# Second feed-forward half of a hybrid layer: direct products over all 512 tokens instead of the seven-product scheme

## Chip, cores and metric

The kernel runs on one core of one Trainium2 chip. The metric is the device time of one execution in microseconds; the kernel before takes 1804.71 us (median of three runs, 1804.62 to 1808.05).

## What is computed

One layer of a diffusion backbone on 512 latent tokens with 256 context tokens, 1,024 features, all in float32: a feed-forward half step, a token mixer (gated DeltaNet and pooling), a second feed-forward half step on the latents alone, and a last RMSNorm. The part that matters here is the second half step and the norm behind it:

```python
def swiglu(h, w_in, w_out):
    g, u = jnp.split(h @ w_in, 2, axis=-1)
    return (jax.nn.silu(g) * u) @ w_out

x = x + mx[5] * mix_x
x = x + 0.5 * mx[8] * swiglu(modulate(rmsnorm(x, norm3_w[i]), mx[6], mx[7]), ffn2_w_in[i], ffn2_w_out[i])
...
return rmsnorm(x, final_norm_w)
```

`w_in` is 1024 x 5632 (2,816 columns for g, 2,816 for u), `w_out` 2816 x 1024.

## The kernel before

Activations lie with the feature on the partition: a tile is 128 features by the tokens. A float32 product is made of three float32r products: each operand is split into a high part (a cast, on ScalarE) and a low part (operand less high part, a subtraction, on VectorE), and TensorE adds high x high, high x low and low x high in PSUM. `split_act` (lines 187 to 189) does this for activations, `halves` (lines 114 to 121) for up to four feature tiles of 128 weight columns (`whi`, `wlo`, four buffers each), `weights` (107 to 112) loads 128 columns of a matrix into a staging buffer `stg` (two of them) by one DMA from SyncE's queue and calls `halves` twice. `job` (123 to 134) is one tile of 128 output features over all tokens: for eight feature tiles, 24 matmuls with 512 columns in one PSUM bank. `next_bank` hands out the eight banks, tagged b, g and a, in turn.

The mixer's last step is eight such jobs with `w_mix_out` (lines 1108 to 1113); each result is added to the residual `xl` (line 1111) and its square to `acc2` (`norm_acc`, 191 to 197), from which `rstd_rows` (199 to 217) makes the norm's factors.

The second half step then goes by pairs of feature tiles. The first pair (lines 1114 to 1128) is made by plain products of 256 columns (`side_by_side`, `plain`), while `modulated` and `blocks_of` make the normalised input; `combine_pair` (on POOL) makes the extra right-hand operands, block differences. All other products go by `quad` (lines 337 to 371): two tiles of 128 output features and two halves of 256 tokens form a 2 x 2 block product, done with seven products instead of eight. The left operands are sums and differences of weight blocks, made on POOL in `quad_weights` (from 292: `qs`, and `qst` in place) and then split by `halves` like any weights; the seven results are added up from PSUM by VectorE (lines 354, 358, 360, 365, 370) and copied by ScalarE (352), into tiles `q`. `ffn` (from line 419) runs the quads in three groups of pairs, `G2 = ((0, 3), (3, 7), (7, 11))`: per pair a quad for g, Silu (line 462), a quad for u, four multiplications (474), and `combine` (252 to 266) with the splits that make seven right-hand operands `ahi`, `alo` for the output product; at the first pair of a group it does the output product of the group before it (`project7`, from 428), four quads, added to `xl` at line 437. Every instruction goes to its engine in an order that the framework's scheduler sets when the program is built; each engine works its own list in that order, and a buffer's next writer waits for its last reader.

After the last output quads `finish` (lines 1141 to 1149) adds the squares, scales by the norm's weight (`xw`, ScalarE), transposes four blocks on TensorE (1148) and copies them to `ot`; then come the row sums (1155), the factor, the scaling and four DMAs to the output.

## Time and profile before

| | |
|---|---|
| runs | 1804.62, 1804.71, 1808.05 us |
| span of the profiled execution | 1807.2 us |
| its own time | not printed apart; of the three runs only 1808.05 isn't shorter than the span, 0.85 us more |
| TensorE, VectorE, ScalarE, POOL busy | 91%, 76%, 52%, 35% of the span |
| chain that ended last | TensorE 55%, VectorE 25%, issue 6%, ScalarE 5%, DMA 5% |
| mean granted TensorE clock | 0.961 |
| DMA | 184 MB, mean 102 GB/s |

How to read it: the shares are means over the whole program, in which the first half step, the mixer and the second half step have different limits. The span is counted from the first to the last instruction. TensorE's matmuls overlap: the time of one in a row (0.28 us and more) is longer than the distance from its start to the next, so rates are read from starts. PEclk is the granted clock, 1.00 for 2.4 GHz and 0.50 for 1.2 GHz.

### The profile page before, as it was taken

What the parts mean: (1) busy time and instruction counts of PE and PEld (TensorE: products, weight loads), DVE (VectorE), ACT (ScalarE), POOL (GpSimd) and SP (SyncE); (2) the same over time, 40 slices, a digit from 0 to 9 for tenths busy, and PEclk for the clock granted to TensorE, in tenths of its full rate; (3) what the DMA queues carried; (4) which work ended last, traced back from release to release, by engine and by line L of the source; (5) the groups of instructions that cost most, each with busy time, mean ns of one, the idle gap of its engine ahead of it and who ended that gap; (6) DMA issues with size and microseconds to landing.
All of it is one profiled execution on the core that took longest, in us unless ns stands there. A gap on an engine that the chain in (4) does not pass through costs nothing.

```text
span 1807.2 us, 34927 instructions
## 1 busy us (share of the span) xinstructions
PE 1649.1 (91%) x13432; PEld 1486.5 (82%) x13432; DVE 1365.7 (76%) x2647; ACT 943.9 (52%) x2088; POOL 632.3 (35%) x669
## 2 busy tenths in 40 slices
PE   6899999999999999899999999999987888888886
PEld 4798998989999778777877888777877888888886
DVE  5778888897878874457776778645549899899886
ACT  5533343434344465757777776564426444444454
POOL 2244434444534020332233321100005556555642
PEclk9999999999999999999999999999998999899988
DMA  9455455351212353522221212247431222222221
GB/s 272 117 147 160 133 144 156 110 161 62 76 59 71 117 169 120 130 64 60 53 59 47 67 40 66 59 132 224 129 105 48 77 88 83 82 82 85 79 82 59
DMA packets 250971, 184.06 MB, mean 102 GB/s; under 512 B 7008, under 2 KB 238133, under 8 KB 250677
## 3 DMA queue, kind: packets, MB, share of 16 engines
q1 hardware_dynamic: 250368, 181.65, 34.4%
q8 instruction: 106, 1.74, 0.4%
q14 instruction: 60, 0.49, 0.1%
q10 hardware_dynamic: 437, 0.18, 0.0%
HBM read 170.22 MB, written 11.58 MB: 101 GB/s over the span
## 4 chain that ended last, share of the span: by engine, by line
PE 55%; DVE 25%; issue 6%; ACT 5%; DMA 5%; POOL 2%; SPq 0%; POOLq 0%; ACTq 0%; DVEq 0%
PE b L132 12%; PE b L345 11%; PE g L345 7%; PE a L345 6%; DVE wlo L120 4%; DVE cv L583 2%; DVE q L474 2%; DVE alo L189 2%; PE b L279 2%; DVE t L257 2%; DVE xT L437 1%; PE a L708 1%; PE a L132 1%; PE b L150 1%; PE g L132 1%
## 5 line engine op out<-in xcount | busy, mean ns | idle before, releaser
L119 ACT CAST whi<-qst 128x512 fp32r<-128x512 f32 (+2 forms) x288 | 159.1, 554 | 164.7 <-PE b L345 66.7
L120 DVE TENSOR_TENSOR wlo<-qst,whi 128x512 fp32r<-128x512 f32 (+2 forms) x288 | 215.5, 757 | 16.7 <-ACT whi L119 16.4
L119 ACT CAST whi<-qs 128x512 fp32r<-128x512 f32 (+2 forms) x216 | 117.7, 554 | 171.4 <-POOL qs L309 82.1
L132 PE MATMUL b<-hhi,whi 128*128 128x512 f32 (+1 forms) x528 | 188.4, 386 | 0.0
L132 PE MATMUL b<-hlo,whi 128*128 128x512 f32 (+1 forms) x528 | 188.3, 385 | 0.0
L132 PE MATMUL b<-hhi,wlo 128*128 128x512 f32 (+1 forms) x528 | 187.7, 386 | 0.0
L308 POOL TENSOR_TENSOR qs<-qst 128x512 f32<-128x512 f32 (+2 forms) x72 | 92.7, 1287 | 253.1 <-DMA qst<-in_ffn_w_in_dram 70.2
L313 POOL TENSOR_TENSOR qs<-qst,qs 128x512 f32<-128x512 f32 (+2 forms) x72 | 87.4, 1214 | 198.1 <-DVE wlo L120 181.1
L119 ACT CAST whi<-stg 128x512 fp32r<-128x512 f32 x154 | 94.3, 620 | 112.7 <-PE b L132 70.4
L120 DVE TENSOR_TENSOR wlo<-qs,whi 128x512 fp32r<-128x512 f32 (+2 forms) x144 | 104.9, 728 | 49.7 <-ACT whi L119 49.4
L345 PE MATMUL b<-ehi,wlo 128*128 128x384 f32 (+1 forms) x240 | 84.3, 351 | 45.7 <-DVE wlo L120 45.7
L179 POOL TENSOR_TENSOR rs<-rs,mhalf 128x4 f32<-128x4 f32 (+2 forms) x13 | 14.0, 1077 | 294.6 <-DVE rs L177 279.0
L188 ACT CAST ahi<-q 128x384 fp32r<-128x384 f32 (+1 forms) x118 | 55.3, 473 | 118.1 <-DVE q L474 60.8
L583 DVE SCALAR_TENSOR_TENSOR cv<-raw,vec,cv 128x772 f32<-128x772 f32 (+1 forms) x96 | 100.4, 1046 | 11.6 <-ACT cv L581 8.3
L345 PE MATMUL g<-hhi,whi 128*128 128x384 f32 (+1 forms) x320 | 105.5, 330 | 2.5 <-ACT whi L119 2.5
L345 PE MATMUL g<-hhi,wlo 128*128 128x384 f32 (+1 forms) x320 | 103.6, 324 | 3.6 <-DVE wlo L120 3.6
L132 PEld LDWEIGHTS b<-hlo,whi 128*128 128x128 f32 x528 | 94.6, 191 | 14.9
L132 PEld LDWEIGHTS b<-hhi,whi 128*128 128x128 f32 x528 | 94.5, 191 | 14.9
L132 PEld LDWEIGHTS b<-hhi,wlo 128*128 128x128 f32 x528 | 94.0, 191 | 15.0
L345 PE MATMUL g<-hlo,whi 128*128 128x384 f32 (+1 forms) x320 | 103.6, 324 | 0.0
L120 POOL TENSOR_TENSOR wlo<-stg,whi 128x512 fp32r<-128x512 f32 x46 | 65.4, 1429 | 90.6 <-ACT whi L119 70.5
L312 POOL TENSOR_TENSOR qst<-qst 128x512 f32<-128x512 f32 (+2 forms) x72 | 95.6, 1327 | 0.6
(480 smaller groups left out, 5459.6 us busy)
## 6 DMA issues: line engine op xcount, KB each, us to landing
qst<-in_ffn_w_in_dram SPq DMA_DIRECT2D x80, 512.0 KB, 3.5
stg<-in_w_ada_dram SPq DMA_DIRECT2D x56, 512.0 KB, 4.6
stg<-in_w_mix_in_dram SPq DMA_DIRECT2D x49, 512.0 KB, 3.9
qst<-in_ffn_w_out_dram SPq DMA_DIRECT2D x40, 256.0 KB, 2.7
adx<-in_w_ada_dram SPq DMA_DIRECT2D x16, 512.0 KB, 7.1
qst<-in_ffn_w_out_dram SPq DMA_DIRECT2D x16, 512.0 KB, 3.8
crow<-cumd SPq DMA_DIRECT2D x16, 384.0 KB, 8.8
stg<-in_ffn_w_in_dram SPq DMA_DIRECT2D x8, 512.0 KB
```

The lines of the kernel that those rows point to most:

```text
L119: (first.copy if first is act else first.tensor_copy)(out=hi[:, :n], in_=w)
L120: second.tensor_tensor(out=lo[:, :n], in0=w, in1=hi[:, :n], op=ALU.subtract)
L132: pe.matmul(res[p][:, :m], lhsT=ww(i), rhs=hh(k)[:, o:o + m], start=(i == 0 and j == 0), stop=(i == n - 1 and j == 2))
L188: act.copy(out=hi, in_=src)
L189: dve.tensor_tensor(out=lo, in0=src, in1=hi, op=ALU.subtract)
L257: eng.tensor_tensor(out=t, in0=x, in1=y, op=ALU.subtract)
L279: pe.matmul(x, lhsT=ww(k), rhs=rhs(j, part, k), start=n + e == 0, stop=n + e == len(ks) + 1)
L308: pool.tensor_tensor(out=s1, in0=a21, in1=a22, op=ALU.add)
L312: pool.tensor_tensor(out=a21, in0=a11, in1=a21, op=ALU.subtract)
L313: pool.tensor_tensor(out=s2, in0=a12, in1=s2, op=ALU.subtract)
L345: pe.matmul(o, lhsT=ww[:, k], rhs=rhs(j, part, k), start=first and k + i == 0, stop=k + i == nh + 1, skip_group_check=not first)
L583: dve.scalar_tensor_tensor(out=cv[:, :n], in0=raw[:, t:t + n], scalar=tap[t], in1=cv[:, :n], op0=ALU.mult, op1=ALU.add)
```

## The change

The second half step no longer uses the seven-product scheme. `tile_weights` loads 128 columns into one of three staging buffers `fst` and splits them into `fhi` and `flo`, five buffers of a whole tile each. The normalised input is written straight into `xhi` and `xlo` (512 tokens each), by one VectorE, one ScalarE and one VectorE step per feature tile. The first two feature tiles' g and u (four weight tiles) are produced while the input comes out, with one 512-column matmul where there were two of 256; every other tile is one `job`. Features go in three groups of tiles, 0 to 7, 8 to 15, 16 to 21; `project_out` adds a group's share to the residual after the first tile of the next group. The helpers `job`, `side_by_side`, `split_act`, `norm_acc`, `rstd_rows` and `finish`'s steps are as before. POOL has no weight sums or block differences left in this half. All other parts of the diff remove comments only.

```diff
-    e2 = ctx.enter_context(tc.tile_pool(name="e2", bufs=1, reuse_waits="tile"))
-    ehi = e2.tile([128, 4 * LAT], F32R, name="ehi2")
-    elo = e2.tile([128, 4 * LAT], F32R, name="elo2")
-    mn_cm = tc.tile_pool(name="mn", bufs=1, reuse_waits="tile")
-    mn = mn_cm.__enter__()
+    mn = ctx.enter_context(tc.tile_pool(name="mn", bufs=1, reuse_waits="tile"))
+    fw = ctx.enter_context(tc.tile_pool(name="fw", bufs=1, reuse_waits="tile"))
+    w_in, w_out = a["ffn2_w_in"], a["ffn2_w_out"]
+    def tile_weights(src, k0, nk, c0):
+        stg = fw.tile([128, KT, 128], F32, tag="fst", name="fst", bufs=3)
+        sp.dma_start(out=stg[:, :nk], in_=src[k0 * 128:(k0 + nk) * 128, c0:c0 + 128].rearrange("(k p) m -> p k m", p=128))
+        hi = fw.tile([128, KT, 128], F32R, tag="fhi", name="fhi", bufs=5)
+        lo = fw.tile([128, KT, 128], F32R, tag="flo", name="flo", bufs=5)
+        for i in range(0, nk, 4):
+            c = slice(i, min(i + 4, nk))
+            split_act(stg[:, c], hi[:, c], lo[:, c])
+        return [(lambda k, w=w: w[:, k]) for w in (hi, lo)]
     for m in range(0, KT, 2):
         for e in range(2):
             r = job(weights(a["w_mix_out"], 0, KT, 128 * (m + e)), lambda k: zhi[:, k], lambda k: zlo[:, k], range(KT), ONLY, next_bank)["lat"]
             dve.scalar_tensor_tensor(out=xl[:, m + e], in0=r, scalar=eff[:, 3, m + e, 0:1], in1=xl[:, m + e],
                                      op0=ALU.mult, op1=ALU.add)
             norm_acc(mn, acc2, xl[:, m + e], m + e, LAT)
-    ws = [weights(a["ffn2_w_in"], 0, KT, c) for c in (0, 128)]
+    hp_cm.__exit__(None, None, None)
+    GROUPS = ((0, 8), (8, 16), (16, 22))
+    hp2 = ctx.enter_context(tc.tile_pool(name="hp2", bufs=1, side="right", reuse_waits="tile"))
+    x2_cm = tc.tile_pool(name="x2", bufs=1, side="right", reuse_waits="tile")
+    x2 = x2_cm.__enter__()
+    xhi = x2.tile([128, KT, LAT], F32R, name="xhi")
+    xlo = x2.tile([128, KT, LAT], F32R, name="xlo")
+    f0 = [tile_weights(w_in, 0, KT, c) for c in (0, FF, 128, FF + 128)]
     for k in range(KT):
         mod_scale(2, k, 7, R_N3)
     mod_gate(1, 8, True)
-    rb = rstd_rows(mn, acc2, ONLY)
-    rhs2 = products(LAT // 2, (ehi, elo))
-    t = {}
-    first = [[[bank(tag)[:, :LAT // 2] for _ in range(2)] for tag in "bg"]]
-    steps = side_by_side(ws, first[0], blocks(rhs2), PAIRED)
-    for n, k in enumerate(PAIRED):
-        t[k] = modulated(mn, rb, xl[:, k], k, 2, 6, ONLY, bufs=8)
-        blocks_of(t[k], k, LAT // 2, rhs2)
+    rb = rstd_rows(mn, acc2, ONLY)["lat"]
+    banks = [bank(tag) for tag in "aagg"]
+    steps = side_by_side(f0, [[b] for b in banks], lambda _, part, k: (xhi, xlo)[part][:, k], range(KT))
+    for k in range(KT):
+        t = mn.tile([128, LAT], F32, tag="nt", name="nt", bufs=2)
+        shift = mods[:, 48 + k, 0:1]
+        dve.scalar_tensor_tensor(out=t, in0=xl[:, k], scalar=eff[:, 2, k, 0:1], in1=rb, op0=ALU.mult, op1=ALU.mult)
+        act.activation(out=xhi[:, k], in_=t, func=AF.Identity, bias=shift)
+        dve.scalar_tensor_tensor(out=xlo[:, k], in0=t, scalar=shift, in1=xhi[:, k], op0=ALU.add, op1=ALU.subtract)
         next(steps)
-    first.append(plain(a["ffn2_w_in"], FF, blocks(rhs2), LAT // 2, tags="ab"))
-    for kp in range(4):
-        combine_pair(mn, t, kp, LAT // 2, rhs2, pool)
-    mn_cm.__exit__(None, None, None)
-    # ---- second half-step and final norm ----
-    with tc.tile_pool(name="fp2", bufs=1, reuse_waits="tile") as fp:
-        late = []
-
-        def room():
-            hp_cm.__exit__(None, None, None)
-            p = ctx.enter_context(tc.tile_pool(name="op", bufs=1, side="right", reuse_waits="tile"))
-            late.append(p)
-            late.append(p.tile([128, 4, D], F32, name="ot"))
-
-        def finish(m):
...
-        ffn(fp, a["ffn2_w_in"], a["ffn2_w_out"], rhs2, ONLY, G2, lambda m: xl[:, m, :],
-            lambda m, s: eff[:, 1, m, s:s + 1], finish, lambda: None, first, 2, room)
+    fp = ctx.enter_context(tc.tile_pool(name="fp2", bufs=1, reuse_waits="tile"))
+    hh = {}
+    def activated(f, g, u):
+        t = fp.tile([128, LAT], F32, tag="ht", name="ht", bufs=2)
+        act.activation(out=t, in_=g, func=AF.Silu)
+        dve.tensor_tensor(out=t, in0=t, in1=u, op=ALU.mult)
+        hh[f] = [hp2.tile([128, LAT], F32R, tag=n, name=n, bufs=10) for n in ("fhhi", "fhlo")]
+        split_act(t, *hh[f])
+    def project_in(f):
+        g, u = (job(tile_weights(w_in, 0, KT, c + 128 * f), lambda k: xhi[:, k], lambda k: xlo[:, k], range(KT), ONLY,
+                    next_bank)["lat"] for c in (0, FF))
+        activated(f, g, u)
+    def project_out(f0, f1, done):
+        for m in range(KT):
+            r = job(tile_weights(w_out, f0, f1 - f0, 128 * m), lambda k: hh[k][0], lambda k: hh[k][1], range(f0, f1), ONLY,
+                    next_bank)["lat"]
+            dve.scalar_tensor_tensor(out=xl[:, m], in0=r, scalar=eff[:, 1, m, 0:1], in1=xl[:, m], op0=ALU.mult, op1=ALU.add)
+            done(m)
+    for f in range(2):
+        activated(f, banks[2 * f], banks[2 * f + 1])
+    for i, (g0, g1) in enumerate(GROUPS):
+        for f in range(max(g0, 2), g1):
+            project_in(f)
+            if f == g0:
+                project_out(*GROUPS[i - 1], lambda m: None)
+    x2_cm.__exit__(None, None, None)
+    op = ctx.enter_context(tc.tile_pool(name="op", bufs=1, side="right", reuse_waits="tile"))
+    ot = op.tile([128, 4, D], F32, name="ot")
...
+    project_out(*GROUPS[-1], finish)
...
```

(What is left out after `project_out(*GROUPS[-1], finish)` and inside `finish` is as in the kernel before, line for line, but for the indentation and the pool's name.)

The scheduler sets each engine's order. The first place is VectorE in the middle of the half. Before, one pair in the second group (`q` from lines 474 and 260, `t` from 257 and 265: products and block differences; `alo`: their low halves; `wlo`: low half of a weight block for the next quad):

```order
L474 TENSOR_TENSOR q<-q 128x256
L257 TENSOR_TENSOR t_19581<-q 128x256
L370 TENSOR_TENSOR q<-q,b 128x256
L260 TENSOR_TENSOR q<-q 128x256
L474 TENSOR_TENSOR q<-q 128x256
L257 TENSOR_TENSOR t_19584<-q,t_19581 128x256
L189 TENSOR_TENSOR alo<-t_19581,ahi 128x256
L189 TENSOR_TENSOR alo<-q,ahi 128x256 x2
L189 TENSOR_TENSOR alo<-t_19584,ahi 128x256
L120 TENSOR_TENSOR wlo<-qst,whi 128x512
```

The same engine in the change, feature tiles 2 to 4 (`ht`: Silu(g) times u; `flo`: low half of half a weight tile; `fhlo`: low half of the activation):

```order
L189 TENSOR_TENSOR fhlo<-ht,fhhi 128x512 x2
L189 TENSOR_TENSOR flo<-fst,fhi 128x512 x8
L1153 TENSOR_TENSOR ht<-ht,b 128x512
L189 TENSOR_TENSOR flo<-fst,fhi 128x512 x2
L189 TENSOR_TENSOR fhlo<-ht,fhhi 128x512
L189 TENSOR_TENSOR flo<-fst,fhi 128x512 x2
L1153 TENSOR_TENSOR ht<-ht,b 128x512
```

Before, nine instructions of the pair stand ahead of a weight block; now each feature tile has one product and one split between the splits of two weight tiles, and the splits of four more tiles stand ahead of the first product.

The second place is TensorE where the first two feature tiles end (line 279, operand `xhi`) and the first jobs begin (line 132), in the change:

```order
L279 MATMUL g<-xhi,fhi 128x512
L279 MATMUL g<-xlo,fhi 128x512
L279 MATMUL g<-xhi,flo 128x512
L132 MATMUL b<-xhi,fhi 128x512
L132 MATMUL b<-xlo,fhi 128x512
L132 MATMUL b<-xhi,flo 128x512
L132 MATMUL b<-xhi,fhi 128x512
L132 MATMUL g<-xhi,fhi 128x512
```

Four matmuls of the job in bank b come first, then all of the job in a bank g, which still holds a result of the first 96 matmuls until ScalarE or VectorE has read it.

The third place is the end of TensorE's list in the change (`xw`: the scaled output, transposed by line 1187):

```order
L132 MATMUL a<-fhhi,fhi 128x512
L132 MATMUL a<-fhlo,fhi 128x512
L132 MATMUL a<-fhhi,flo 128x512
L1187 MATMUL b<-ident,xw 128x128 x8
L132 MATMUL b<-fhhi,fhi 128x512
L132 MATMUL b<-fhlo,fhi 128x512
L132 MATMUL b<-fhhi,flo 128x512
```

The transposes of two output tiles stand between the last matmuls of one job and the first of the last one; before, transposes stood in fours between the products of a quad, and the last eight behind all of them.

## Rows read from the trace of the kernel before

**Rows 1.** The page, part 1: busy us, share of the span, instructions by engine.

```profile
PE 1649.1 (91%) x13432; PEld 1486.5 (82%) x13432; DVE 1365.7 (76%) x2647; ACT 943.9 (52%) x2088; POOL 632.3 (35%) x669
```

**Rows 2.** Busy time by stretch: us, PE, PEld, DVE, ACT, POOL, PEclk, DMA, GB/s.

```profile
1302.80:1347.40 44.60, 44.60 (x192) 35.84 (x191) 21.72 (x32) 14.88 (x24) 0.00 (x0) 1.00 0.33 94
...
1358.90:1363.60 4.70, 4.63 (x21) 4.63 (x22) 4.65 (x9) 4.70 (x12) 3.35 (x5) 0.50 0.02 5
...
1358.90:1792.40 433.50, 373.06 (x2820) 365.50 (x2820) 390.82 (x608) 212.63 (x439) 238.50 (x175) 0.91 0.24 75
...
1528.70:1535.10 6.40, 6.40 (x57) 6.40 (x56) 6.33 (x11) 2.88 (x6) 4.34 (x4) 1.00 0.26 82
...
1540.00:1544.00 4.00, 4.00 (x19) 4.00 (x20) 3.94 (x9) 1.96 (x4) 0.00 (x0) 0.50 0.45 131
...
1769.00:1773.00 4.00, 4.00 (x22) 4.00 (x23) 4.00 (x4) 3.04 (x6) 3.92 (x3) 0.61 0.00 0
```

**Rows 3.** Waits from 1347 to 1808: us in total, times, longest us.

```profile
PE b L345 <- DVE wlo L120: 40.8, 11, 4.8
```

**Rows 4.** Timeline of TensorE around a pause: start us, us, instruction, wait before it.

```profile
1528.73 0.28 PE L345 MATMUL a<-hhi,whi 128*128 128x256 f32 x1
...
1535.19 0.28 PE L345 MATMUL b<-elo,whi 128*128 128x256 f32 x1
...
1539.98 0.58 PE L345 MATMUL b<-ehi,wlo 128*128 128x256 f32 x1 [4.51 <-DVE wlo L120]
...
1540.36 0.41 PE L345 MATMUL b<-ehi,whi 128*128 128x256 f32 x1
...
1544.41 0.36 PE L345 MATMUL g<-hlo,whi 128*128 128x256 f32 x1
```

**Rows 5.** Chain of waits through that pause: start us, us, engine, tile, line.

```profile
1535.16 1.41 DVE q L474
...
1536.57 1.41 DVE t L257
...
1539.32 0.61 DVE wlo L120
```

**Rows 6.** Chain of waits, the mixer's output projection, first and last of eight jobs.

```profile
1302.83 5.62 PE g L132 x24
...
1342.18 5.63 PE b L132 x24
```

**Rows 7.** Timeline of TensorE, last part of the projection before it, first and last.

```profile
1284.76 0.39 PE L132 MATMUL g<-yghi,wlo 128*128 128x512 f32 x1
...
1302.44 0.39 PE L132 MATMUL b<-yghi,wlo 128*128 128x512 f32 x1
```

**Rows 8.** Chain of waits from 1300 to 1810: a table load, matmuls on `ahi`.

```profile
1382.12 1.28 ACT L462
...
1460.66 1.08 PE g L345 x9
```

**Rows 9.** Groups by line, 1302.5 to 1347.5: busy us, mean ns, idle before.

```profile
L120 DVE TENSOR_TENSOR wlo<-stg,whi 128x512 fp32r<-128x512 f32 x16 | 11.0, 687 | 8.5 <-ACT whi L119 8.5
...
L119 ACT CAST whi<-stg 128x512 fp32r<-128x512 f32 x16 | 9.9, 621 | 25.8 <-PE b L132 13.4 <-PE a L132 6.8 <-PE g L132 5.5
...
L1111 DVE SCALAR_TENSOR_TENSOR xl<-b,eff,xl 128x512 f32<-128x512 f32 x3 | 2.3, 751 | 5.0 <-PE b L132 5.0
```

**Rows 10.** Loads of line 110, 1230 to 1350, from issue to landing.

```profile
DMA to landing us min/median/max: 3.0/3.4/3.9
```

**Rows 11.** Chain of waits at the start of the half.

```profile
1357.11 1.52 ACT nt L225 x2
...
1358.63 0.30 ACT hhi L188
...
1358.97 0.58 PE b L279
```

**Rows 12.** Timeline of TensorE, the last matmul of the half.

```profile
1792.19 0.28 PE L345 MATMUL b<-ahi,wlo 128*128 128x256 f32 x1
```

More of the change, by code (lines that the diff above doesn't have):

```diff
@@ L1128, in layer_kernel @@
-    for kp in range(4):
-        combine_pair(mn, t, kp, LAT // 2, rhs2, pool)
-    mn_cm.__exit__(None, None, None)
-    with tc.tile_pool(name="fp2", bufs=1, reuse_waits="tile") as fp:
-        late = []
-        def room():
-            hp_cm.__exit__(None, None, None)
-            p = ctx.enter_context(tc.tile_pool(name="op", bufs=1, side="right", reuse_waits="tile"))
-            late.append(p)
-            late.append(p.tile([128, 4, D], F32, name="ot"))
-        def finish(m):
-            p, ot = late
-            norm_acc(p, acc2, xl[:, m], m, LAT)
-            y = p.tile([128, LAT], F32, tag="xw", name="xw", bufs=2)
-            act.activation(out=y, in_=xl[:, m], func=AF.Copy, scale=vec[:, 0, R_NF + m:R_NF + m + 1])
-            b = bank()
-            for c in range(4):
-                pe.transpose(b[:, c * 128:(c + 1) * 128], y[:, c * 128:(c + 1) * 128], ident)
-            act.copy(out=ot[:, :, m * 128:(m + 1) * 128], in_=b.rearrange("p (c x) -> p c x", c=4))
-        ffn(fp, a["ffn2_w_in"], a["ffn2_w_out"], rhs2, ONLY, G2, lambda m: xl[:, m, :],
-            lambda m, s: eff[:, 1, m, s:s + 1], finish, lambda: None, first, 2, room)
+    rb = rstd_rows(mn, acc2, ONLY)["lat"]
@@ L1153, in layer_kernel, with finish @@
+    x2_cm.__exit__(None, None, None)
+    op = ctx.enter_context(tc.tile_pool(name="op", bufs=1, side="right", reuse_waits="tile"))
+    ot = op.tile([128, 4, D], F32, name="ot")
+    def finish(m):
+        norm_acc(op, acc2, xl[:, m], m, LAT)
+        y = op.tile([128, LAT], F32, tag="xw", name="xw", bufs=2)
+        act.activation(out=y, in_=xl[:, m], func=AF.Copy, scale=vec[:, 0, R_NF + m:R_NF + m + 1])
         b = bank()
         for c in range(4):
-            pe.matmul(b[:, c:c + 1], lhsT=acc2[:, c * 128:(c + 1) * 128], rhs=ones[:, 0:1])
@@ L1156, in layer_kernel @@
-        r = rstd_of(b[:, :4], 4, D)
-        ot = late[1]
-        for c in range(4):
-            if c % 2:
-                act.activation(out=ot[:, c], in_=ot[:, c], func=AF.Copy, scale=r[:, c:c + 1])
-            else:
-                dve.tensor_scalar(out=ot[:, c], in0=ot[:, c], scalar1=r[:, c:c + 1], scalar2=None, op0=ALU.mult)
-            sp.dma_start(out=out[0, c * 128:(c + 1) * 128, :], in_=ot[:, c])
+            pe.transpose(b[:, c * 128:(c + 1) * 128], y[:, c * 128:(c + 1) * 128], ident)
@@ new lines, in finish @@
+        act.copy(out=ot[:, :, m * 128:(m + 1) * 128], in_=b.rearrange("p (c x) -> p c x", c=4))
+    project_out(*GROUPS[-1], finish)
+    b = bank()
+    for c in range(4):
+        pe.matmul(b[:, c:c + 1], lhsT=acc2[:, c * 128:(c + 1) * 128], rhs=ones[:, 0:1])
+    r = rstd_of(b[:, :4], 4, D)
+    for c in range(4):
+        if c % 2:
+            act.activation(out=ot[:, c], in_=ot[:, c], func=AF.Copy, scale=r[:, c:c + 1])
+        else:
+            dve.tensor_scalar(out=ot[:, c], in0=ot[:, c], scalar1=r[:, c:c + 1], scalar2=None, op0=ALU.mult)
+        sp.dma_start(out=out[0, c * 128:(c + 1) * 128, :], in_=ot[:, c])
```

## Prediction, made before the changed kernel was run

> **What bounds the kernel now.** I read the engine totals first: TensorE is busy for 91% of the span, VectorE for 76% [rows 1]. An average over stages doesn't say what the second half waits for, so the table of stretches comes next [rows 2]. From 1358.9 to 1792.4 us, the feed-forward half itself, TensorE is busy for 373.06 of 433.50 us at a mean granted clock of 0.91, VectorE for 390.82: there VectorE is the fuller engine. The table of waits of that stretch names the place: TensorE stood 40.8 us before matmuls of bank b, 11 times, each time for `wlo` of line 120, the low half of a weight tile that VectorE splits off [rows 3]. The timeline shows one such pause [rows 4]: matmuls follow one another until 1535.19, the next starts at 1539.98, after 4.51 us of waiting. The chain of waits says what VectorE did meanwhile [rows 5]: the pair's multiplications and block differences (`q`, `t`, 1.4 us each though only 256 wide), and only after them `wlo`. They stand ahead of it in VectorE's order.
>
> The pause costs twice. After it the matmuls start 0.213 us apart instead of 0.117 [rows 4], because the granted clock of 1540.0 to 1544.0 is 0.50, the 1.2 GHz level, where 1528.7 to 1535.1 shows 1.00, the 2.4 GHz level [rows 2]. From 1540.36 to 1544.41 lie 19 such steps, then the distance is short again; at half rate for some 4.6 us some 2.1 us are lost, so a pause of 4.5 us costs about 6.6.
>
> **How 433 us are made up.** The seven-product scheme issues 2,796 matmuls of 256 columns here: 192 for the first pair by plain products, 20 quads of 84 for `w_in` (1,680), 4 quads of 63 and 8 of 84 for `w_out` (924). 55 steps lead from 1528.73 to 1535.19 [rows 4], 0.1174 us each: 2,796 x 0.1174 = 328 us at the full clock. TensorE's idle time is 433.5 - 373.1 = 60 us. The rest, 433.5 - 328 - 60 = 45 us, is half clock and the 32 transposes of the end. So 105 us of the stage are not matmuls at full speed.
>
> **What the change does, part by part.**
>
> 1. Matmuls: 44 tiles of `w_in` x 8 feature tiles x 3 = 1,056 and 8 x 22 x 3 = 528 for `w_out`, 1,584 of 512 columns. The same shape, from the same kind of job (one 512 KB weight load, two casts, two subtractions, 24 matmuls), runs just ahead of the stage, in the output projection of the mixer: eight jobs in a row of 5.62 or 5.63 us without a gap [rows 6], 0.2344 each, clock 1.00 for 44.6 us [rows 2]. 1,584 x 0.2344 = 371.3 us, **43 us more** matmul time than before. The rows bound this price: 79 starts from 1284.76 to 1302.44 (the projection before, operand `yghi`) are 0.2267 apart [rows 7], so down to 359.1; nine 256-wide matmuls on `ahi` take 1.08 us [rows 8], 0.24 per 512, so up to 380. I take 0.2344, of the nearest stage; nothing in the rows says why they differ. The Trainium skill (TensorE: Matmul & The Clock Gate, section "Back-to-back issue gap") gives N/2.4 + 2.5 ns, 216 ns for 512 columns; by it the sum would be 30 us lower. The trace disagrees by 19 ns a matmul, and the measurement decides.
>
> 2. VectorE and POOL: gone are the block differences and the sums of weights. VectorE keeps 136 subtractions of 512-wide weights at 0.687, 22 products, 22 splits and 24 residual updates of about 0.7 to 0.75 [rows 9]: some 142 us in 371. ScalarE: 136 + 22 casts at 0.62 and 22 Silus of about that, some 112 us. Per tile of 5.62 us VectorE needs about 2.1, ScalarE 1.9. In the new VectorE order the splits of four tiles stand ahead of the first product, splits run about four tiles ahead of their use, and a product that waits for TensorE does not make TensorE wait. I cost these edits at nothing; the cover is those four tiles, 22 us. If it were gone, a tile's cast, subtraction and hand-overs (about 1.7 us) would be bare.
>
> 3. Weight loads: as many bytes, 512 KB per 5.62 us, 93 GB/s. The mixer's output projection moves the same at 94 GB/s [rows 2] in packets half as long as those of the old `qst` loads, each landing in 3.0 to 3.9 us [rows 10]. Nothing. Five of the loads and their ten splits now run inside that projection: 10 x 0.69 us more on VectorE, which is busy 21.72 of 44.60 us there [rows 2]. Hidden, unless a weight load of the projection falls behind them; then one pause, up to 6.6.
>
> 4. Start: from the last matmul of the projection (1347.81) to the first of the half it takes 11.2 us, through norm and row factors [rows 11]. The new code has one ScalarE step where there were two in a row (`nt` x2, `hhi`): first matmul at about 1358.0, 0.9 earlier. VectorE and ScalarE then feed a feature tile about every 1.7 us, TensorE needs 2.8 for its 12 matmuls. The clock starts at 0.50 as before [rows 2]: 4.7 us of it, 2.1 lost. When the first 96 matmuls end, the banks g are free only after a table load (1.28 [rows 8]) and two Silus: 0.7.
>
> 5. End: eight jobs of 18 matmuls, with 28 of the 32 transposes between them (0.5 for four, 3.5 in all). Each needs its residual update and a ScalarE copy, some 2.5 us after its job; the order puts 9 to 18 matmuls between, but the last two rounds stand bare: waits of about 3.5 in all, and 2 for the clock that falls (it read 0.61 from 1769 to 1773, between the same rounds of the old end [rows 2]). From the last matmul's start, 1792.19, the old tail takes 15.0 to the span's end [rows 12]; its steps are the same.
>
> **The sum**: 10.2 + 371.3 + 2.1 + 0.7 + 3.5 + 3.5 + 2.0 = 393.3 after 1347.8, so the last matmul is at 1741.1, the span's end at 1756.1, against 1807.2: 51.1 less. Put otherwise, of the 105 us of pauses, half clock and transposes some 12 stay, and 43 are paid back in columns. The span is 2.5 above the median of the runs, 1804.7; 1804.7 - 51.1 = **1753.6 us**.
>
> **Rivals.**
> - *The matmul rate of the projection before.* If the rows at 0.2267 hold for the new operands, which lie like `yghi` in rows of 512 tokens, it is 12.2 less: 1741. For it: they are the one other stretch of this shape; against it: all 192 matmuls nearest to the change ran at 0.2344.
> - *No overhead at all.* At half clock 256 columns take 0.2132 [rows 4], just 256 / 1.2 GHz; at twice the clock 512 would take the same, 33.6 us less: 1720. No stretch in the trace shows it. The page's rule above belongs here, with 1724.
> - *A few pauses remain* (at the hand-over from the first 96 matmuls, at the two group borders, in the projection ahead, at the end): two to five of 6.6 us, 1767 to 1787. Against it: the projection had none in eight jobs, with only two tiles of look-ahead.
> - *Slower: TensorE pauses at the borders of jobs and falls to 1.2 GHz.* The place is the VectorE order where `ht` waits for a finished bank and the next `flo` stands behind it. If look-ahead fails there once a feature tile, 20 pauses cost 132 us: 1886. It decides from eight pauses on (8 x 6.6 = 53). For it: it is just what bounds the stage now. Against it: the four tiles of cover, VectorE at 2.1 of 5.6 us, and 44.6 us without a gap across eight banks. The Trainium skill (the same page, section "A second HAM failure mode: psum-queue depth-cycling") tells of a kernel at N = 512 whose clock swung as it cycled through PSUM banks. That rule speaks against this change; the trace disagrees, with clock 1.00 over eight such jobs.
>
> **How the numbers follow.** My forecast, 1744 to 1765, has 0.60: the sum, with the tail's waits gone or doubled. The faster rate has 0.15, no overhead 0.03, remaining pauses 0.15, something between those and no change 0.03, slower 0.04. 1737 to 1776 holds the forecast, the faster rate and about half of the pauses; 0.17 stays out. About 0.2% (3.6 us) is what a measurement of this kernel can tell from no change. Faster 0.95, same 0.01, slower 0.04.
>
> **What would show it.** Right: in the changed kernel the jobs of the half take 5.6 us for 24 matmuls, TensorE's waits for `flo` are near nothing, the clock reads 1.00 from about 1363 until the last rounds, VectorE is busy under half of the stage. Wrong: 5.44 or 5.76 us a job (rate), pauses of several us before a tile's first matmul (splits or loads), or the stretch 1303 to 1348 getting longer (the early loads).

## The result, and the profile after

The changed kernel took 1753.05 us (median of 4 runs, 1749.31 to 1756.71), the kernel before beside it 1806.38 (4 runs): a ratio of 0.9697, 95% interval 0.9673 to 0.9721. The forecast was 1753.6, faster. The profiled execution took 1756.71 us, its span is 1755.0, the longest of the four (the others 1747.6 to 1751.7).

The engine totals of the changed kernel, from its page, answer to [rows 1]:

```profile
PE 1653.5 (94%) x12220; PEld 1423.9 (81%) x12220; DVE 1119.0 (64%) x2254; ACT 842.6 (48%) x1851; POOL 390.8 (22%) x493
```

VectorE lost 247 us of work, POOL 242; TensorE's busy time is nearly the same (4 us more). The table of stretches (columns as in [rows 2]):

```profile
1307.60:1352.50 44.90, 44.90 (x192) 35.80 (x191) 25.49 (x39) 18.18 (x31) 0.00 (x0) 1.00 0.56 152
...
1358.00:1363.00 5.00, 3.18 (x5) 1.41 (x6) 2.70 (x5) 1.38 (x2) 0.00 (x0) 0.50 0.00 0
1384.00:1700.00 316.00, 316.00 (x1350) 253.88 (x1349) 112.69 (x176) 89.49 (x162) 0.00 (x0) 1.00 0.33 95
1735.00:1742.00 7.00, 4.88 (x23) 3.70 (x22) 1.44 (x2) 1.84 (x4) 0.00 (x0) 1.00 0.00 0
...
1358.00:1742.00 384.00, 379.28 (x1614) 302.74 (x1614) 138.71 (x217) 111.75 (x200) 0.00 (x0) 0.99 0.27 80
```

Over the half TensorE is busy for 379.28 of 384.00 us at clock 0.99, and from 1384 to 1700 without a break at 1.00; before, it was busy for 373.06 of 433.50 at 0.91 [rows 2]. VectorE needs 138.71 us of the half (390.82 before), POOL none (238.50). The early loads fall into the mixer's output projection (first row: 152 GB/s where there were 94), and TensorE has no gap there.

What is left of the pauses stands in the table of waits from 1300 to 1756 (us in total, times, longest), all of TensorE's entries; [rows 3] is gone:

```profile
PE b L1187 <- ACT xw L1184: 4.3, 3, 2.2
PE b L215 <- DVE diag L209: 2.3, 1, 2.3
PE b L205 <- DVE acc L197: 2.3, 1, 2.3
PE a L279 <- ACT xhi L1143: 1.6, 1, 1.6
```

The chain of waits shows the half from its first to its last matmul (start us, us, engine, bank, line, count):

```profile
1361.90 1.22 PE a L279 x2
...
1386.87 0.93 PE b L132 x4
1387.80 5.72 PE g L132 x24
1393.52 4.69 PE b L132 x20
...
1696.21 5.62 PE b L132 x24
1701.84 4.22 PE g L132 x18
...
1736.31 0.66 PE b L1187 x4
1736.96 4.23 PE b L132 x18
1741.19 0.02 issue
```

A job is 5.62 us, and one follows the other without a gap until 1733.59. In the profiled pair the half takes 1755.0 - 1352.58 = 402.4 us from the end of the mixer's projection, where it took 1807.2 - 1347.81 = 459.4 [rows 6]: 57.0 less. That the projection ended 4.8 us later hides a part of it in the spans. In the profiled runs below the same job ended between 1344.7 and 1355.3, so a few us of a difference in whole time can lie ahead of the half.

### The profile page after: what moved, and what is told of

The parts are those of the page before. It is cut to its first block, busy times and chain, and to the rows that moved or that the text cites. A ratio compares the mean times of both kernels' runs of the same rounds, so it can differ in the third digit from the quotient of the medians.

```text
span 1755.0 us, 31315 instructions
## 1 busy us (share of the span) xinstructions
PE 1653.5 (94%) x12220; PEld 1423.9 (81%) x12220; DVE 1119.0 (64%) x2254; ACT 842.6 (48%) x1851; POOL 390.8 (22%) x493
## 4 chain that ended last, share of the span: by engine, by line
PE 71%; DVE 14%; ACT 5%; DMA 5%; POOL 2%; issue 2%; SPq 0%; ACTq 0%; POOLq 0%; DVEq 0%
PE b L132 22%; PE b L345 9%; PE a L132 6%; PE g L132 6%; PE a L345 5%; PE g L345 5%; DVE cv L583 2%; PE b L279 2%; PE a L279 1%; PE g L279 1%; PE a L708 1%; ACT din L848 1%; DVE wlo L120 1%; DMA bg_dram<-bgate 1%; PE b L150 1%
## 5 line engine op out<-in xcount | busy, mean ns | idle before, releaser
L188 ACT CAST fhi<-fst 128x512 fp32r<-128x512 f32 (+1 forms) x136 | 77.7, 605 | 249.6 <-PE b L132 85.6
L189 DVE TENSOR_TENSOR flo<-fst,fhi 128x512 fp32r<-128x512 f32 (+1 forms) x136 | 87.3, 671 | 92.6 <-ACT fhi L188 92.4
L119 ACT CAST whi<-qst 128x512 fp32r<-128x512 f32 (+1 forms) x160 | 81.6, 512 | 106.5 <-PE b L345 43.2
L119 ACT CAST whi<-qs 128x512 fp32r<-128x512 f32 (+1 forms) x120 | 59.5, 512 | 115.2 <-POOL qs L309 76.2
L120 DVE TENSOR_TENSOR wlo<-qst,whi 128x512 fp32r<-128x512 f32 (+1 forms) x160 | 100.7, 639 | 10.1 <-ACT whi L119 10.0
L120 DVE TENSOR_TENSOR wlo<-stg,whi 128x512 fp32r<-128x512 f32 x100 | 68.2, 686 | 22.1 <-ACT whi L119 20.2
L120 DVE TENSOR_TENSOR wlo<-qs,whi 128x512 fp32r<-128x512 f32 (+1 forms) x80 | 49.0, 613 | 32.6 <-ACT whi L119 32.6
L132 PE MATMUL b<-xlo,fhi 128*128 128x512 f32 x160 | 63.4, 396 | 0.0
L132 PE MATMUL b<-xhi,flo 128*128 128x512 f32 x160 | 63.4, 396 | 0.0
L132 PE MATMUL b<-xhi,fhi 128*128 128x512 f32 x160 | 63.4, 396 | 0.0
```

Source lines behind the costliest of these rows:

```text
L119: (first.copy if first is act else first.tensor_copy)(out=hi[:, :n], in_=w)
L120: second.tensor_tensor(out=lo[:, :n], in0=w, in1=hi[:, :n], op=ALU.subtract)
L132: pe.matmul(res[p][:, :m], lhsT=ww(i), rhs=hh(k)[:, o:o + m], start=(i == 0 and j == 0), stop=(i == n - 1 and j == 2))
L188: act.copy(out=hi, in_=src)
L189: dve.tensor_tensor(out=lo, in0=src, in1=hi, op=ALU.subtract)
```

## The experiments

Theory as predicted: VectorE's work per pair stands ahead of the next split, so TensorE pauses and restarts at half clock; the change ends that and pays 43 us of columns. Rivals: fewer matmuls are the gain; the number of weight buffers is; POOL is. Ratios are to the kernel before on the same chip in the same session; the changed kernel's own is 0.9697.

| kernel | median us | ratio (95%) |
|---|---|---|
| changed, jobs in two halves of 256 | 1755.55 | 0.9701 (0.9686 to 0.9715) |
| before, no block differences | 1768.27 | 0.9777 (0.9761 to 0.9793) |
| before, six weight buffers | 1788.91 | 0.9879 (0.9863 to 0.9895) |
| before, no sums on POOL | 1724.22 | 0.9538 (0.9511 to 0.9565) |
| before, POOL's sums unread | 1821.96 | 1.0066 (1.0040 to 1.0091) |
| changed, POOL kept busy | 1763.29 | 0.9750 (0.9719 to 0.9781) |
| changed, operands moved | 1742.62 | 0.9626 (0.9599 to 0.9653) |
| changed, weights moved | 1741.10 | 0.9627 (0.9599 to 0.9655) |
| changed, both moved | 1748.55 | single run, no interval |
| mixed, seven products for `w_in` | 1754.31 | 0.9692 (0.9678 to 0.9707) |
| mixed, for the gate half only | 1745.61 | 0.9651 (0.9624 to 0.9677) |
| mixed, gate half, moved operands | 1743.99 | 0.9636 (0.9618 to 0.9654) |

The three kernels without block differences, without POOL's sums and with the sums unread compute something else in the half, from as many matmuls; only their times are read.

### Is it the number of matmuls?

```diff
+        for s in range(2):
+            c = slice(256 * s, 256 * s + 256)
+            for i, k in enumerate(ks):
+                for j, (ww, hh) in enumerate(((w[0], act_hi), (w[0], act_lo), (w[1], act_hi))):
+                    pe.matmul(b[:, c], lhsT=ww(i), rhs=hh(k)[:, c], start=(i == 0 and j == 0), stop=(i == n - 1 and j == 2))
```

> The changed kernel with each job's 512 tokens again as two runs of 256-column matmuls, one token half after the other in the same bank (1,488 of the 1,584 matmuls; the first 96 stay). Same columns, same splits and buffers, but 3,072 matmuls in place of 1,584. Theory (the gain is pauses and half clock that went): two matmuls of 0.117 take the place of one of 0.234, 5.6 us a job, no pauses, the time of the changed kernel, 1745 to 1760. Rival (the gain comes from half as many matmuls and weight loads on TensorE): a good part of the 50 us comes back, 1780 or more.

Measured 0.9701, the same as the changed kernel. Twice the matmuls and weight loads in these jobs cost nothing that the intervals show; that rival is out.

### Less work for VectorE, or more look-ahead?

The products that read the differences read plain blocks instead (left out), and the differences aren't made:

```diff
-                    combine(fp, g[0][0], g[0][1], g[1][0], g[1][1], n2, put, deep - 1)
+                    if final:
+                        combine(fp, g[0][0], g[0][1], g[1][0], g[1][1], n2, put, deep - 1)
```

> The kernel before, second half only, without the block differences of the activations and their splits; the products that would read them read one of the blocks instead (so the second half computes something else, with the same 2,796 matmuls). VectorE loses eight operations a pair, nothing else changes. Theory (VectorE's chain of a pair stands ahead of the next split, TensorE pauses and then runs at half clock): the waits for the low half of a weight tile shrink from 41 us to under 10, the clock of the half rises from 0.91 to 0.97 or more, 1740 to 1765. Rival (fewer matmuls and weight loads are the gain): the matmuls are as many as before, so 1795 to 1806. Rival (the number of split-weight buffers): the buffers are as before, so 1790 to 1806.

The other one takes two more `whi` and `wlo` buffers from the half's own pool:

```diff
+        more[1] += 1
+        p, nb = (more[0], 2) if more[0] and more[1] % 6 >= WB else (wp, WB)
+        hi = p.tile([128, 4, 128], F32R, tag="whi", name="whi", bufs=nb)
+        lo = p.tile([128, 4, 128], F32R, tag="wlo", name="wlo", bufs=nb)
```

> The kernel before, with six instead of four buffers for the split weights in the second half, nothing else. Theory (VectorE's work per pair, 390 of 433 us, and its order): VectorE has little idle time to run ahead in, so the gain is small, 1785 to 1806. Rival (the look-ahead in buffers is what lacks): the pauses of 4.5 us go, since two more products of 1.4 us are split ahead, 1750 to 1770.

Without the block differences some 40 us went, with the buffers 21.5: the first lies 3 us above the theory's range, the second inside it. But not every sign came as expected. Without the differences TensorE still waited 18.7 us for `wlo`, where under 10 were expected. With six buffers the wait of [rows 3] did go, as the rival had it; others took its place, mainly for VectorE's sums of the seven products (waits from 1340 to 1790):

```profile
PE a L349 <- DVE q L362: 23.8, 25, 2.0
```

So both the order and the look-ahead mattered, and VectorE stayed behind in either. What it did is the interesting part. Stretches of the run without differences, and its split (groups by line, 1359 to 1760: busy us, mean ns, idle before):

```profile
1347.00:1765.00 418.00, 365.47 (x2863) 350.05 (x2861) 375.56 (x541) 201.55 (x407) 248.65 (x178) 0.97 0.28 86
```

```profile
L120 DVE TENSOR_TENSOR wlo<-qst,whi 128x512 fp32r<-128x512 f32 (+1 forms) x128 | 144.8, 1136 | 7.5 <-ACT whi L119 7.1
```

Eight operations a pair are gone, and VectorE is still busy for 375.56 of 418 us: its split takes 1136 ns here, in a group with a few of 384 columns (932 in the same view of the kernel before); those of 128x512 alone take 1166 (936 before), where [rows 9] has 687. So the number of VectorE's operations is not all that filled it. Something made them long.

### What makes VectorE's operations long

The timeline of the kernel before through the pause of [rows 5], VectorE and then POOL (start us, us, instruction):

```profile
1533.98 1.18 DVE L260 TENSOR_TENSOR q<-q 128x256 f32<-128x256 f32 x1
1535.09 1.49 DVE L474 TENSOR_TENSOR q<-q 128x256 f32<-128x256 f32 x1
1536.50 1.48 DVE L257 TENSOR_TENSOR t<-q,t 128x256 f32<-128x256 f32 x1
1537.90 0.41 DVE L189 TENSOR_TENSOR alo<-t,ahi 128x256 fp32r<-128x256 f32 x1
...
1533.52 1.36 POOL L308 TENSOR_TENSOR qs<-qst 128x512 f32<-128x512 f32 x1
1534.96 1.33 POOL L309 TENSOR_TENSOR qs<-qs,qst 128x512 f32<-128x512 f32 x1
1536.25 1.44 POOL L312 TENSOR_TENSOR qst<-qst 128x512 f32<-128x512 f32 x1
```

Each of the three long operations ends 0.28 to 0.29 us after a POOL instruction does (1534.88, 1536.29, 1537.69), one after the other; from 1537.90, with POOL at rest, the same width takes 0.41.

The trace shows the same all through the half of the kernel before. From 1358.9 to 1792.4, 137 of VectorE's operations on two tiles of the on-chip memory took over 0.1 us longer than alone. Every one of them ended a fixed time after the end of a POOL instruction that fell inside it: 0.28 or 0.29 us at 256 columns, 0.41 or 0.42 at 384, 0.55 or 0.56 at 512. Of the 177 with one input in PSUM none was longer, though 95 of them ran beside POOL. (22 more two-tile ones overlapped a POOL instruction and kept their time.) So an operation that is held up stands still until POOL's instruction is over. The next two runs separate that from POOL's place in the chain of data.

First POOL's four sums and differences a quad are left out (parts of the edit):

```diff
+        if plain:
+            s1, s2 = a22, a12
+        else:
+            pool.tensor_tensor(out=s1, in0=a21, in1=a22, op=ALU.add)
...
-        pool.tensor_tensor(out=s2, in0=a12, in1=s2, op=ALU.subtract)
```

> The kernel before, second half only, without POOL's four sums and differences of weight blocks per quad; the products that would read them read plain blocks of the weights (so the second half computes something else, with the same 2,796 matmuls and the same number of splits, casts and block differences of activations). VectorE's instructions are the same to the last one; only POOL's busy time in the half falls, from 238 us to about 50. Theory (VectorE's own number of operations fills it): its 390 us stay, and the time stays within 10 us of the kernel before, 1795 to 1812. Rival (VectorE is slow because POOL works beside it: 128x256 operations take 0.41 us where POOL rests and 1.0 to 1.5 where it doesn't): VectorE's operations fall to 0.69 and 0.41, some 290 us in all, the pauses shrink to a third, 1745 to 1770.

Then they are made again, into a tile that nothing reads (two of the four):

```diff
+            d = tmp.tile([128, 4, 128], F32, tag="pd", name="pd", bufs=1)[:, :nh]
+            pool.tensor_tensor(out=d, in0=a21, in1=a22, op=ALU.add)
+            pool.tensor_tensor(out=d, in0=a12, in1=a11, op=ALU.subtract)
...
```

> The kernel before, second half only, with the plain blocks of weights as in the run without POOL's sums, but with POOL doing its four additions and subtractions per quad again, from the same tiles into a tile that nothing reads (so the second half computes something else). No product waits for POOL's results any more; POOL's work beside VectorE is back. Theory after the run without POOL's sums, contention (VectorE is slow while POOL works): VectorE's 128x256 operations are back at 1.0 us and more, the pauses come back, 1785 to 1810. Rival, dependence (the way from load over POOL's sums to the split was too long, with two buffers for a sum): the pauses stay away, 1720 to 1740.

Without POOL's sums the seven-product kernel takes 1724 us, 84 less than before, below even the rival's range, and the changed kernel's direct products are 29 slower than that. So the theory that VectorE's own number of operations fills it is out. With the sums back, read by nobody, it takes 1822, more than the kernel before and 12 above the range expected. So the dependence on the sums is worth little, and that they run beside VectorE is most of the 84 us. Stretches and groups (1359 to 1792) without the sums:

```profile
1347.00:1717.00 370.00, 347.07 (x2847) 341.51 (x2846) 305.31 (x627) 220.56 (x450) 60.40 (x50) 0.97 0.31 96
```

```profile
L120 DVE TENSOR_TENSOR wlo<-qst,whi 128x512 fp32r<-128x512 f32 x168 | 113.5, 685 | 16.7 <-ACT whi L119 15.4
...
L480 DVE TENSOR_TENSOR q<-q 128x256 f32<-128x256 f32 x30 | 12.6, 421 | 0.7
```

And with the sums unread, the same two views and the wait that is back:

```profile
1347.00:1820.00 473.00, 379.06 (x2873) 366.40 (x2871) 416.47 (x631) 222.41 (x453) 243.51 (x178) 0.92 0.25 76
```

```profile
L120 DVE TENSOR_TENSOR wlo<-qst,whi 128x512 fp32r<-128x512 f32 x164 | 165.0, 1019 | 11.4 <-ACT whi L119 11.3
L486 DVE TENSOR_TENSOR q<-q 128x256 f32<-128x256 f32 x30 | 24.8, 826 | 0.7
```

```profile
PE b L357 <- DVE wlo L120: 40.5, 10, 5.1
```

The same instructions on VectorE (627 and 631 in the two stretches) take 305 us beside a POOL that works for 60, and 416 beside one that works for 244. The wait of [rows 3], 40.8 us in 11 pauses, is there again with 40.5 in 10. One thing differs from the kernel before: TensorE now also waits 12.7 us, in 11 pauses, for weight splits that POOL makes itself (`wlo` from POOL), where the kernel before has no long wait for POOL. That is not VectorE's slowness, and may be why this run is slower than the kernel before.

Then the other way round, POOL busy in the changed kernel:

```diff
+        d = fw.tile([128, 512], F32, tag="pd", name="pd", bufs=1)
+        for i in range(3):
+            pool.tensor_tensor(out=d, in0=stg[:, 0:4].rearrange("p k m -> p (k m)"), in1=stg[:, 1:5].rearrange("p k m -> p (k m)"), op=ALU.add)
```

> The changed kernel with three additions of 128x512 on POOL for every weight tile of the half, into a tile that nothing reads: POOL works for about 4.3 of each 5.6 us. Theory of the prediction (splits run four tiles ahead, VectorE needs 2.1 of 5.6 us): even if VectorE's splits take 1.0 to 1.1 instead of 0.69 us it keeps ahead, 1750 to 1760, no pauses. Rival (a POOL that rests is the whole gain): the pauses come back, 1780 or more. If POOL does not slow VectorE at all, its split stays at 0.69 us here, and the rival of the run without POOL's sums has lost its reason.

Groups of this run by line (1359 to 1792), and its stretch behind the start:

```profile
L189 DVE TENSOR_TENSOR flo<-fst,fhi 128x512 fp32r<-128x512 f32 x118 | 133.3, 1160 | 43.2 <-ACT fhi L188 43.1
L189 DVE TENSOR_TENSOR fhlo<-ht,fhhi 128x512 fp32r<-128x512 f32 x22 | 35.7, 1627 | 0.0
L1156 DVE TENSOR_TENSOR ht<-ht,b 128x512 f32<-128x512 f32 x20 | 13.8, 688 | 54.3 <-PE b L132 54.3
```

```profile
1365.00:1738.00 373.00, 371.20 (x1586) 297.42 (x1585) 214.93 (x211) 108.11 (x195) 265.03 (x180) 1.00 0.28 82
```

Splits take 1160 and 1627 ns instead of 686 and 684. The product `ht`, of the same shape, one of whose inputs is a PSUM bank (`b`), takes 688 as in a quiet kernel: what POOL holds up is the operation that reads two tiles of the on-chip memory. The Trainium skill has this as a rule (SBUF — State Buffer, section "Who interferes with whom"): a VectorE instruction with two inputs in SBUF contends with a GpSimd instruction that reads SBUF, and one with at most one such input, outside the 2-port perf modes, does not; the port pair that the two engines share is an exclusive lock. The traces agree: 1160 against 688 ns here, and the ends 0.28 us behind POOL's in the pause.

The time rose by some 10 us only, 3 above the range of the look-ahead theory and far below the rival's 1780, for VectorE at 214.93 of 373 us keeps ahead. TensorE stood for 1.8 us in that stretch; the rest is mostly two waits, 5.8 us together, in the projection ahead, where early splits, 1.7 us long, stood before the projection's own. So a busy POOL is dear where VectorE is nearly full, and cheap where it isn't.

### Where a job's 5.62 us come from

In the traces a job of 24 matmuls takes 5.44 us on `yghi` and 5.62 on `hhi`, `xhi` and the activations. The first lie in a pool taken from the low end of the on-chip memory, like all weights; the others in one taken from the high end.

The edit moves the operands' two pools to the low end (`side="right"` is the high one):

```diff
-    hp2 = ctx.enter_context(tc.tile_pool(name="hp2", bufs=1, side="right", reuse_waits="tile"))
-    x2_cm = tc.tile_pool(name="x2", bufs=1, side="right", reuse_waits="tile")
...
+    hp2 = ctx.enter_context(tc.tile_pool(name="hp2", bufs=1, reuse_waits="tile"))
+    x2 = ctx.enter_context(tc.tile_pool(name="x2", bufs=1, reuse_waits="tile"))
```

> The changed kernel with the operands that stream through TensorE (the normed input, 32 KB per partition, and the activations, 40 KB) allocated from the other end of the on-chip memory, where the weights lie too. Same instructions. Jobs on operands from that end take 5.44 us in the traces (yghi in every kernel, and the output jobs of the mixed version), on operands from the end where they lie now 5.62 us. Theory (where the operand lies sets the step of 0.2267 or 0.2344 us): 5.44 us a job, 12 us less than the changed kernel, 1738 to 1745. Rival (the step is set by something else, such as the operations beside it): 5.62 us, 1748 to 1758.

Then the weights too, with the operands low, and with the operands high as in the changed kernel:

```diff
-    fw = ctx.enter_context(tc.tile_pool(name="fw", bufs=1, reuse_waits="tile"))
...
     hp_cm.__exit__(None, None, None)
+    fw = ctx.enter_context(tc.tile_pool(name="fw", bufs=1, side="right", reuse_waits="tile"))
```

> The version with the streamed operands at the other end, where its jobs took 5.44 us, but now with the weights moved as well, to the end where the operands were: the two have changed places. (The weights' tiles now wait for the mixer's operands to be released, so the half starts some 10 us later; only the time of a job is read here.) Theory (the place of the streamed operand alone sets the step): 5.44 us a job. Rival (operands and weights at the same end are fast, at two ends slow): 5.62 us a job.

> The changed kernel with the weights moved to the end where the streamed operands lie; the operands stay. (The weights' tiles wait for the mixer's operands to be released, so the half starts some 6 to 10 us later.) So far, by ends of operand and weights: both at the low end 5.44 us a job, operand high and weights low 5.62, operand low and weights high 5.60. Theory (one end for both is fast): 5.44 us a job, and 1742 to 1752 in all. Rival (only the low end for both is fast): 5.60 us or more a job, 1752 to 1765.

One job from the chain of waits of each: operands low and weights low; operands low, weights high; both high.

```profile
1403.60 5.44 PE g L132 x24
```

```profile
1457.13 5.60 PE a L132 x24
```

```profile
1390.22 5.44 PE a L132 x24
```

Both low 5.44, both high 5.44, apart 5.60 or 5.62. The first theory (the place of the operand alone) fell with the second run; that jobs are fast when operand and weights lie at the same end fits all four combinations. Which addresses count isn't shown, nor why. Two combinations give kernels that beat the changed one: 0.9626 and 0.9627, with intervals that end below 0.9673, where its own begins. From the end of the projection their profiled halves take 392.8 and 393.5 us, against 402.4. (The late start that was expected with the weights moved did not come: the first matmul follows the projection by 9.6 and 9.3 us, in the changed kernel by 9.3.)

### Versions to beat both

Seven products where they are cheap, direct products where the block differences are. First for all of `w_in`, with `w_out` direct:

```diff
+                r = job(weights(w_out, f0, f1 - f0, 128 * m), lambda k: hh[k][0], lambda k: hh[k][1], range(f0, f1), ONLY,
...
-        ffn(fp, a["ffn2_w_in"], a["ffn2_w_out"], rhs2, ONLY, G2, lambda m: xl[:, m, :],
...
+        ffn_out_direct(fp, a["ffn2_w_in"], a["ffn2_w_out"], rhs2, ((0, 4), (4, 8), (8, 11)), finish, first, room)
```

> A mixed version, to beat both: w_in by the seven-product scheme as in the kernel before (1,872 matmuls of 256 columns), w_out by direct products of 512 columns as in the changed kernel (528), so no block differences of the activations; nine buffers for split weights, pairs in groups of four, four and three. TensorE: 1,872 x 0.1174 + 528 x 0.2344 = 343.5 us, 28 less than the changed kernel. VectorE needs about 19 us per pair of feature tiles, where TensorE takes 31. Theory (only VectorE's chain of block differences made the pauses): 1720 to 1740, clock near 1.00. Rival (any work of VectorE between two splits makes them, also the 12 short ones of the scheme's sums): a pause and half clock of some 5 us in each of 20 quads, 1800 or more. Rival (fewer matmuls are the gain): 2,400 matmuls lie between the two kernels, 1775 to 1790.

No better than the changed kernel. A pause stays in most pairs; one in the timeline, and VectorE's split by groups (1340 to 1760):

```profile
1535.18 0.39 PE L349 MATMUL a<-hhi,whi 128*128 128x256 f32 x1 [2.18 <-DVE q L362]
```

```profile
L124 DVE TENSOR_TENSOR wlo<-qst,whi 128x512 fp32r<-128x512 f32 x80 | 88.8, 1113 | 9.3 <-ACT whi L123 8.3
```

The theory that the block differences alone made the pauses falls: they are gone, and pauses stay. POOL's sums for the remaining quads keep the splits at 1113 ns; that this is what leaves the pauses, which are for VectorE's sums (`q`), is argued and not tested. Half as many quads, the gate's alone (against the version just shown):

```diff
-            seq += [(w_in, 256 * pr), (w_in, FF + 256 * pr)]
+            seq += [(w_in, 256 * pr)]
...
+                    u = up(weights(w_in, 0, KT, FF + 256 * pr + 128 * i))
```

> A second mixed version: seven products for the gate half of w_in alone, direct products for its other half (256 columns each, from the same blocks) and for w_out (512 columns); nine buffers for split weights. TensorE: 1,992 matmuls x 0.1174 + 528 x 0.2267 = 353.6 us, 18 less than the changed kernel. Half as many quads, so half the sums on POOL and half the short sums on VectorE per pair of the first mixed version, which had a pause of about 2 us in every pair. Theory (VectorE and POOL must leave room): few pauses, clock above 0.98 in the half, 1730 to 1742. Rival (each quad brings a pause however few there are): 10 pauses of 2 us and their half clock, 1760 or more.

TensorE is busy for 250 of 250 us from 1450 to 1700: no pause any more. The time is still 4 us above the range expected. The direct jobs of 256 columns take 5.68 us, though, and from 1365 to 1450, while POOL makes the input's block differences, TensorE idles for 4.6 us. The last version gives these jobs 512 columns of operands at the low end, and makes the input's differences on VectorE beside two direct pairs:

```diff
+                if pr > 1:
+                    src = quads(lambda j, part, k: rhs[j][part][:, k], n2)
...
+                    u = direct(FF + 256 * pr + 128 * i) if pr else first[1][i]
```

> A third version: seven products for the gate half of w_in from the third pair of feature tiles on, direct 512-column products for all the rest, with the streamed operands at the fast end; the block differences of the input are made on VectorE while the first two pairs run direct. Nine quads of 9.87 us take the place of 18 direct jobs of 5.44: 9 x 1.0 = 9 us less than the version with moved operands (1742.6), if no pause comes. Theory (9 quads leave VectorE and POOL enough room): 1730 to 1738. Rival (POOL's sums beside VectorE bring pauses even so): 1742 or more.

0.9636: as good as the moved operands alone, not better, and 6 us above the theory's range. From 1450 to 1700 there is again no pause; most of the 9 us went into two waits at the start. The first is for a ScalarE cast that stood behind the casts of the differences and the Silus after them, the second for a split behind two VectorE operations of 1.75 us beside POOL:

```profile
PE g L136 <- ACT whi L123: 5.1, 1, 5.1
...
PE g L136 <- DVE wlo L124: 2.6, 1, 2.6
```

So the best versions are the two with operands and weights at one end, some 12 us below the changed kernel. Not tried: the full seven-product scheme with its sums of weights made somewhere else than on POOL, which the run without any sums puts at 1724 us at best.

## Why the prediction held, and where it was incomplete

**The size.** In the profiled pair the half became 57.0 us shorter, forecast 51.1. Term by term, from the end of the projection: the start 1361.90 - 1352.58 = 9.3 (10.2); the first 96 matmuls 24.97 us where 22.5 are at full clock, so half clock cost at most 2.5 (2.1); the hand-over, 48 matmuls in 11.34 where 11.25 are due, 0.1 (0.7); jobs 5.62 us, 0.2343 a matmul (0.2344); the transposes on the chain 2.9 (3.5); one bare stretch at the end, 1733.59 to 1736.31, 2.7 (3.5); the clock at the end read 1.00 from 1735 to 1742, so nothing (2.0), which was luck, see below; from the last job's end to the span's end 13.8, some 14.0 from its last matmul (15.0). Every term but one was a little too large; together they make up nearly all of the 5.9 us by which the half beat its forecast. The later end of the projection in the profiled run took 4.8 back. The median is nearer to the forecast than its parts deserve.

The term for the clock is the one that luck decided. The three versions with moved pools have the same end, with a bare stretch of 2.7 to 2.8 us before the last job, and there the clock did fall. Their last 18 matmuls took 5.40, 5.17 and 5.75 us, where the jobs before took 4.1 to 4.2, and the granted clock read 0.70 from 1721 to 1726 with the operands moved. The longest, with the weights moved:

```profile
1718.71 5.75 PE b L132 x18
```

So some 1.0 to 1.6 us of the 2.0 are real in those executions, and were missing in the profiled one of the changed kernel.

**What held.** The price of a matmul, taken from the stage next door (0.2344) and not from the projection before that (0.2267), with the reason left open; the moved operands show that 0.2267 was to be had. It was the right one of the two, by the runs with moved pools, because the new operands lie at the high end, as those of the stage next door do, and `yghi` does not. The prediction went by nearness and did not know this, so the choice was in part luck. The look-ahead of four tiles: no wait for `flo`, even with splits of 1.2 to 1.6 us. The early loads: hidden, though one busier engine was enough to show them (5.8 us with POOL at work). None of the rivals came. The Trainium skill's rule that spoke against the change (TensorE: Matmul & The Clock Gate, section "A second HAM failure mode: psum-queue depth-cycling"), told there of bf16, did not show with these operands: the clock read 1.00 over 316 us, in some 56 jobs that change banks.

**What was incomplete.** The step on the pause: it said that VectorE's operations of 1.4 us, "though only 256 wide", stand ahead of `wlo` in VectorE's order. That is so, but the question in that half sentence was not followed. They take 0.41 us; the rest is waiting for POOL, whose sums the same change removes. The prediction named POOL's work as gone and priced it at nothing, beside VectorE's shorter list. On the seven-product kernel, taking away the sums alone is worth 84 us, taking away VectorE's block differences alone 40. The two overlap and can't be added. For the changed kernel both are gone, so its time came out the same. With POOL put back to work there, all but some 10 us of the gain stayed, so VectorE's shorter list alone carried most of it in that run: what the prediction said of the change holds. As an explanation of the 105 lost microseconds before, VectorE's own list was the smaller part. The step also left another change unseen, to keep the cheaper products and rest POOL; whether the sums can be had elsewhere at that price wasn't tried.

## What to carry to other kernels

When an operation takes three times as long as its width explains, find what runs beside it before counting operations: here VectorE's two-tile operations waited for POOL, and some 130 instructions (178 against 50) on an engine that none of TensorE's long waits named took 84 us with them when they went. Offloading to POOL is dear when VectorE is nearly full and reads both inputs from the on-chip memory. Where matmuls bound a stage, try operands and weights in pools at the same end: 3% of each matmul for the side of one pool.

## What the runs showed of the hardware

- VectorE operations with two tile inputs that a POOL instruction held up ended a fixed time after it, 0.28 us at 256 columns, 0.41 at 384, 0.55 at 512, in all 137 cases of the half before: up to 1.50 us instead of 0.41 at 256 columns. With one input in PSUM they keep their time (688 ns beside a POOL at work for 265 of 373 us).
- A 512-column matmul starts every 0.2267 us when operand and weights lie at the same end, every 0.2333 to 0.2344 when they don't; two matmuls of 256 columns cost as much as one of 512 at 0.2344 (5.62 us a job in both).
- After the bare stretch at the end, 2.7 us long, the clock read 1.00 from 1735 to 1742 in the changed kernel, and 0.70 over 5 us behind a like stretch in the version with moved operands; the pause of 4.5 us in [rows 4] was followed by 0.50 [rows 2].
